# A gated MLP on one core: the fallback path rewritten as loops, another order for the last output tile, and fewer, wider warm-up matmuls

## The chip, the cores and the metric

The kernel runs on one NeuronCore of a Trainium2 chip. The metric is the device time of one execution in microseconds (us). The profile shows one execution, and its "span" runs from the first to the last recorded instruction of that execution. The time is some 1.5 to 1.9 us longer than the span, in four runs of one kernel (short, below) 2.1 to 2.7 us. The runs were made in several sessions, and the record names different chips for them; each ratio compares with runs of the kernel before of the same session. In the views, PE and PEld are TensorE's matmuls and weight loads, DVE is VectorE, ACT ScalarE, POOL GpSimd, and SPq the queue of SyncE, which issues most of the DMA transfers (80 of 86 in the kernel before). To evict a product is to copy it from the tile that TensorE wrote to the output tile `o`.

## The reference

```python
# x: 16 x 256 x 512, w1: 512 x 4096, w2: 2048 x 512, all float32, normal random numbers
h = x @ w1
gate, value = np.split(h, 2, axis=-1)
h = np.maximum(gate, 0) * value
return (h @ w2).astype(np.float32)
```

## The kernel before

The kernel has two ways through the work. The fast way computes everything in float16 with a seven-product scheme for 2 x 2 blocks (products P1 to P7), and at the same time sums squares of the inputs to decide whether float16 is fit for them. A branch at the end reads the verdict. With the inputs of this case it always jumps over the general way, which is therefore compiled but never executed.

```python
    with ExitStack() as fast:
        unfit = fast_way(fast, tc, x2, w1, w2, out2, flag)
    with tc.If(unfit > 0, label="general"):
        with ExitStack() as general:
            general_way(general, tc, x2, w1, w2, out2)
```

The general way is unrolled in Python: 8 chunks of 512 rows, each with 16 transposes, 128 first-layer matmuls and 64 second-layer matmuls.

```python
    for c in range(T // TH):                       # TH = 512
        xt = xp.tile([P, NK, TH], F32R, name="g_xt", tag="g_xt")
        for b in range(TH // P):
            t = xp.tile([P, D], F32, name="g_t", tag="g_t")
            nc.gpsimd.dma_start(out=t, in_=x2[c * TH + b * P:c * TH + (b + 1) * P, :])
            # ... 4 transposes and copies
        # ... for h in range(NH): 8 matmuls each;  for b in range(TH // P): 16 matmuls each, output by nc.gpsimd.dma_start
```

At its start, the fast way keeps TensorE busy on zeros while the first loads are under way. At its end, it computes the last of the four output tiles of the last 1,024 rows ("pair 3") in an order of its own. Each product that completes a quarter of an output is evicted by ScalarE or VectorE, and SyncE sends it.

```python
    for i in range(NWARM):                         # NWARM = 24
        nc.tensor.matmul(Y[:, :P], warm_b[:, :P], warm_b[:, :P], start=True, stop=True)
    nc.tensor.matmul(Y, warm_b[:, :P], warm_b, start=True, stop=True)
    # ...
    LAST_ORDER = ORDER.replace("P5 3, P2 3, P6 3, P3 3, P7 3", "P2 3, P6 3, P5 3, P7 3, P3 3")   # then P4 3
    # ...
            job(84, lambda: tc.mark_branch_hint_location("general", "LikelyTaken", [ENG.PE, ENG.DVE, ENG.SP]))
```

The last line asks for a hint that the branch around the general way will be taken. In the trace TensorE executes it once, at 0.82 us, some 300 us ahead of the branch.

## Time and profile before

| | |
|---|---|
| time, median of the first 3 runs | 308.26 us (307.19 to 308.72) |
| span of the profile | 307.2 us |
| last matmul ends | 303.03 us |
| tail: from there to the end of the span | 4.13 us |

The head and the chain of waits of the profile page of the kernel before:

```profile
span 307.2 us, 5283 instructions
...
PE 301.6 (98%) x1905; PEld 184.2 (60%) x1905; DVE 236.0 (77%) x388; ACT 176.3 (57%) x348; POOL 151.2 (49%) x189
...
PE 96%; DMA 2%; SPq 1%; issue 0%; ACT 0%
```

TensorE is the chain of waits, and nothing but the first microseconds and the last four can be moved by a change that leaves all products as they are.

The start of the timeline of the kernel before (start in us, length in us, engine, line, operation, tiles, and what the engine waited for):

```profile
0.24 0.10 POOL L774 MEMSET const-float32-0.0<- 128x1 f32 x1 [0.24 <-issue]
...
0.85 0.87 SPq L488 DMA_DIRECT2D x_A<-in_x_dram  x2
...
1.28 2.74 PE L148 MATMUL Y<-warm 128*128 128x128 f16 x24 [1.28 <-DVE warm L144]
```

The end of the timeline of the kernel before: the last eviction on ScalarE and the last three outputs issued by SyncE.

```profile
301.84 0.33 SPq L370 DMA_DIRECT2D out_dram<-o  x1
...
302.65 0.33 SPq L370 DMA_DIRECT2D out_dram<-o  x1
...
303.07 0.38 ACT L405 ACTIVATE o<-Y 128x256 f32<-128x256 f32 x1 [2.24 <-PE Y L362]
...
303.48 1.34 SPq L370 DMA_DIRECT2D out_dram<-o  x1
```

The last issue takes four times as long as the two before it. The DMA view of the kernel before, for 302 to 309 us (GB/s in 40 equal slices of 0.175 us; then queues with packets, MB and share; then issues with the time to landing):

```profile
GB/s 0 0 0 35 322 322 164 0 135 363 199 6 18 18 12 18 18 12 6 293 351 100 0 0 0 0 0 0 0 0 0 0 0 0 0 0 0 0 0 0
...
q8 instruction: 1, 0.02, 1.2%
q14 instruction: 1, 0.01, 0.4%
...
out_dram<-o SPq DMA_DIRECT2D x3, 128.0 KB, 2.7
```

Besides the outputs, there are instruction fetches, the packets of the queues that the view calls "instruction": one of 16 KB on queue 8 and one of 8 KB on queue 14. The trace's single packet records, below the views, place the 16 KB packet at 303.15 to 304.44 us. From 304 to 305.3 us the GB/s row shows 6 to 18 GB/s, where the outputs before and after it reach 351 to 363 in a slice. In the packet records, 14 of the 16 completion writes (packets of 4 bytes) of the output issued at 302.65 us come by 303.99 us, the last two at 304.73 and 305.14 us: as I read it, one or two late DMA engines are working off their packets alone. SyncE's closing wait for outputs, from the view of waits of SyncE's own queue in the same window (us in total, times, longest us):

```profile
SPq L785 <- DMA out_dram<-o: 0.4, 1, 0.4
```

### The profile page before, as it was taken

The page shows a single profiled execution, that of the slowest core. Times are in us where ns is not written, and L with a number is a line of the kernel's source. Part 1 is how long each engine was busy: PE and PEld are TensorE (multiplying, and loading weights), DVE is VectorE, ACT ScalarE, POOL GpSimd, SP SyncE. Part 2 cuts the span into 40 slices and gives each one's busy share as a digit, 9 for nine tenths or more (in the row PEclk, how much of TensorE's full clock was granted, in tenths as well). Part 3 has the DMA queues.
Part 4 walks back from the last instruction along what each step waited for, and adds up shares of the span by engine and source line. Part 5 has one row for each costly group of instructions (what it writes and reads, how often), then busy time and mean ns, then how long its engine had stood idle before and what let it go on. Part 6 is the DMA issues. An engine that isn't in the chain of part 4 may idle for free.

```text
span 307.2 us, 5283 instructions
## 1 busy us (share of the span) xinstructions
PE 301.6 (98%) x1905; PEld 184.2 (60%) x1905; DVE 236.0 (77%) x388; ACT 176.3 (57%) x348; POOL 151.2 (49%) x189
## 2 busy tenths in 40 slices
PE   8999999999999999999999999999999999999994
PEld 7744444588844444478864444458884444447883
DVE  2579888899778888887538888888536888888851
ACT  2488896455865555537855555546866555553231
POOL 2389999800068999300029889700007988700000
PEclk9999999999999999999999999999999999999999
DMA  6985779965775270001354910000325110001132
GB/s 204 358 259 179 239 171 176 229 123 80 260 209 88 69 137 3 0 0 55 136 182 108 207 34 2 0 2 9 130 101 174 35 34 0 3 1 34 54 106 87
DMA packets 35836, 32.87 MB, mean 107 GB/s; under 512 B 14432, under 2 KB 31328, under 8 KB 35680
## 3 DMA queue, kind: packets, MB, share of 16 engines
q1 hardware_dynamic: 33536, 26.22, 28.3%
q0 software_dynamic: 2272, 6.29, 11.4%
q8 instruction: 16, 0.26, 0.4%
q14 instruction: 12, 0.10, 0.1%
HBM read 27.26 MB, written 12.58 MB: 130 GB/s over the span
## 4 chain that ended last, share of the span: by engine, by line
PE 96%; DMA 2%; SPq 1%; issue 0%; ACT 0%
PE Y L250 26%; PE X L250 17%; PE W L250 17%; PE Y L362 14%; PE W L362 9%; PE X L362 9%; DMA x_A<-in_x_dram 2%; PE X L325 1%; PE W L325 1%; PE Y L325 1%; PE Y L498 0%; PE X L498 0%; SPq L217 0%; SPq L488 0%; ACT o L405 0%
## 5 line engine op out<-in xcount | busy, mean ns | idle before, releaser
L250 PEld LDWEIGHTS <-w_T 128*128 128x128 f16 x496 | 48.3, 98 | 57.3 <-POOL w_T L232 1.1
L179 POOL TENSOR_TENSOR fold<-xh 128x1024 f32<-128x1024 f16 x16 | 30.3, 1894 | 94.6 <-DMA xh<-x 93.7
L250 PE MATMUL X<-x_A,w_B 128*128 128x512 f16 x248 | 73.8, 379 | 0.0
L250 PE MATMUL Y<-x_S,w_T 128*128 128x512 f16 x220 | 65.5, 379 | 0.0
L250 PEld LDWEIGHTS <-w_B 128*128 128x128 f16 x372 | 36.3, 98 | 42.1
L277 DVE SCALAR_TENSOR_TENSOR cc<-W,pu 128x512 f32<-128x512 f32 x62 | 42.9, 691 | 21.1 <-ACT pu L271 21.1
L257 ACT COPY Y<-X 128x512 f32<-128x512 f32 x62 | 35.4, 571 | 38.2 <-PE X L250 37.9
L271 ACT ACTIVATE pu<-Y 128x512 f32<-128x512 f32 x62 | 37.1, 598 | 33.9 <-PE Y L250 33.0
L182 POOL TENSOR_TENSOR fold<-fold 128x512 f32<-128x512 f32 (+2 forms) x96 | 51.8, 539 | 7.5
L362 PEld LDWEIGHTS <-w_stage 128*128 128x128 f16 x512 | 50.0, 98 | 5.9
L287 DVE SCALAR_TENSOR_TENSOR cc<-Y,pu 128x512 f32<-128x512 f32 x62 | 42.9, 691 | 6.7
L282 DVE SCALAR_TENSOR_TENSOR g<-X,cc 128x512 f16<-128x512 f32 x62 | 42.8, 691 | 2.3
L299 DVE SCALAR_TENSOR_TENSOR g<-Y,cc 128x512 f16<-128x512 f32 x62 | 42.2, 681 | 1.8 <-PE Y L250 1.8
L362 PEld LDWEIGHTS <-g 128*128 128x128 f16 x384 | 37.5, 98 | 8.2
L264 ACT ACTIVATE pu<-W 128x512 f32<-128x512 f32 x62 | 37.2, 600 | 0.8 <-PE W L250 0.6
L250 PE MATMUL W<-x_S,w_B 128*128 128x512 f16 x124 | 36.9, 379 | 0.0
L250 PE MATMUL W<-x_S,w_T 128*128 128x512 f16 x124 | 36.9, 379 | 0.0
L250 PE MATMUL Y<-x_A,w_T 128*128 128x512 f16 x124 | 36.9, 379 | 0.0
L362 PE MATMUL X<-w,g 128*128 128x256 f16 x256 | 31.9, 273 | 0.0
L394 DVE SCALAR_TENSOR_TENSOR o<-W,pu 128x256 f32<-128x256 f32 x16 | 6.8, 423 | 19.4 <-PE W L362 19.4
L169 DVE TENSOR_TENSOR w_stage<-g 128x1024 f16<-128x1024 f16 x32 | 21.4, 684 | 0.2
L232 POOL TENSOR_TENSOR w_T<-w_stage 128x512 f16<-128x512 f32 (+1 forms) x16 | 18.7, 1173 | 2.5 <-DMA w_stage<-in_w_dram 2.5
(100 smaller groups left out, 307.5 us busy)
## 6 DMA issues: line engine op xcount, KB each, us to landing
w_stage<-in_w_dram SPq DMA_DIRECT2D x14, 512.0 KB, 6.0
out_dram<-o SPq DMA_DIRECT2D x26, 256.0 KB, 2.1
x<-in_x_dram POOLq DMA_DIRECT2D x4, 1024.0 KB, 9.1
xh<-x SPq DMA_DIRECT2D x16, 256.0 KB, 3.0
w<-in_w_dram POOLq DMA_DIRECT2D x2, 1024.0 KB, 10.2
out_dram<-o SPq DMA_DIRECT2D x12, 128.0 KB, 1.7
w_stage<-in_w_dram SPq DMA_DIRECT2D x4, 256.0 KB, 5.4
x_S<-in_x_dram SPq DMA_DIRECT2D x4, 256.0 KB, 6.5
```

The costliest lines, as they stand in the source:

```text
L169: eng.tensor_tensor(o[n], o[i0], o[i1], op=op)
L179: nc.gpsimd.tensor_tensor(fold, t, t, op=MULT)
L182: nc.gpsimd.tensor_tensor(fold[:, :, :m], fold[:, :, :m], fold[:, :, m:2 * m], op=ADD)
L250: nc.tensor.matmul(ps, wop[wn][:, b, self.jb * P:(self.jb + 1) * P], self.xo[xn][:, b, :], start=fresh and b == 0, stop=b == 1, skip_group ...
L257: nc.scalar.copy(out=self.Y, in_=self.X)
L264: nc.scalar.activation(self.p5, self.W, COPY, scale=GS)
L271: nc.scalar.activation(self.u2, self.Y, COPY, scale=GS)
L277: nc.vector.scalar_tensor_tensor(out=self.c12, in0=self.W, scalar=GS, in1=self.u2, op0=MULT, op1=ADD)
L282: nc.vector.scalar_tensor_tensor(out=self.g[:, self.jb, :TH], in0=self.X, scalar=0.0, in1=self.c12, op0=MAX, op1=MULT)
L287: nc.vector.scalar_tensor_tensor(out=self.c22, in0=self.Y, scalar=GS, in1=self.p5, op0=MULT, op1=ADD)
L299: nc.vector.scalar_tensor_tensor(out=self.g[:, self.jb, TH:], in0=self.Y, scalar=0.0, in1=self.c22, op0=MAX, op1=MULT)
L362: nc.tensor.matmul(ps, self.op[an][:, i], vop[wn][:, i], start=name in ("P1", "P5") and i == 0, stop=i == NJ // 2 - 1, skip_group_check=True)
```

## The change

Its intent was to make the code that is skipped small, to issue fewer TensorE instructions for the same warm-up time, and to send the last tile's outputs at better times. The diff, cut to its core:

```diff
-NWARM = 24
+NWARM = 4 * [TH] + 8 * [P]
 ... in general_way
-    for c in range(T // TH):
-        xt = xp.tile([P, NK, TH], F32R, name="g_xt", tag="g_xt")
+    xt = wp.tile([P, NK, TH], F32R, name="g_xt")
+    g = wp.tile([P, NH, TH], F32R, name="g_g")
+    with tc.For_i(0, T, TH) as row:
         for b in range(TH // P):
-            nc.gpsimd.dma_start(out=t, in_=x2[c * TH + b * P:c * TH + (b + 1) * P, :])
+            nc.gpsimd.dma_start(out=t, in_=x2[bass.ds(row + b * P, P), :])
 ...
-        for h in range(NH):
+        with tc.For_i(0, NH, 1) as h:
 ...
-            nc.gpsimd.dma_start(out=out2[c * TH + b * P:c * TH + (b + 1) * P, :], in_=o)
+            nc.gpsimd.dma_start(out=out2[bass.ds(row + b * P, P), :], in_=o)
 ... in fast_way
-    for i in range(NWARM):
-        nc.tensor.matmul(Y[:, :P], warm_b[:, :P], warm_b[:, :P], start=True, stop=True)
+    for n in NWARM:
+        nc.tensor.matmul(Y[:, :n], warm_b[:, :P], warm_b[:, :n], start=True, stop=True)
 ...
-    LAST_ORDER = ORDER.replace("P5 3, P2 3, P6 3, P3 3, P7 3", "P2 3, P6 3, P5 3, P7 3, P3 3")
+    LAST_ORDER = ORDER.replace("P5 3, P2 3, P6 3, P3 3, P7 3", "P6 3, P5 3, P7 3, P2 3, P3 3")
```

The output tile `o` is now allocated by whichever of P2 and P7 comes first.

## The prediction

> **What bounds it.** By the chain of waits TensorE is 96% of the span of 307.2 us, one DMA (x_A landing at 8.2 us) 2%. From 8.25 us to the last matmul's end at 303.03 us the timeline shows TensorE practically without gaps, so no product is saved. The change can only touch the head (8.2 us, bound by that load) and the tail: 4.1 us from the last matmul to the end of the span.

> **The tail, from the timeline and the raw instruction and packet records.** ScalarE's last eviction ends at 303.45; SyncE starts the last output's issue at 303.48, and that issue takes 1.34 us, where the two before it took 0.33 us. Its last packet is at 305.84 us, 2.36 us after the start of the issue; the two before needed 1.34 us. SyncE's closing waits and barriers add 1.3 us. What stands in the way: a 16 KB packet on the instruction queue, 303.15 to 304.44 us, right after TensorE's compare-and-branch (301.89 us) jumped over the unrolled general way. [...]packets of the output before are late as well (305.14 us). Likewise the issue at 299.11 took 1.04 us, fetch at 298.45.

> These fetches come about every 250 recorded TensorE instructions[...].

> **What the change does.**
> 1. Looped general way: never executed, but the code the branch skips shrinks on TensorE from some 3,300 instructions to about 200. I expect the target in the block already fetched, so the fetch at 303.15 us goes away. The last issue then takes 0.33 us instead of 1.34: about -1.0 us, all on the critical path.
> 2. Warm matmuls: 3,584 columns before and after (with the closing 512), so the same 2.9 us; 12 fewer pairs, 24 fewer TensorE instructions. The trace's full clock starts at 6.3 us, before the x_A load at 8.2. Direct gain 0. It shifts the block boundaries by 24 instructions: the last sequential fetch moves by 12 x 0.109 = 1.3 us, to about 299.8 us, and helps the branch and its target to share a block.
> 3. Last pair P6 P5 P7 P2 P3 P4: same products, same end of TensorE at 303.0. P6 follows the copy of X to Y with only P4 2 between; the copy ended at 297.37, P6 would start at 297.67, so no bubble. P2's output moves from 299.1 to about 301.7, P7's forward from 301.8 to about 300.97, away from the fetch; P3's and P4's stay. The last output decides, so 0 by itself.

> **Sum.** Span 307.2 to about 306.1 us if the late fetch goes (I give it two in three), unchanged if the branch still enters a new block. Predicted time 307.4 us, range 306.4 to 308.5 (the three runs of before spread over 1.5 us). Faster by over 2%: 0.02; within 2%: 0.965; slower by over 2%: 0.015.

> **Right or wrong in the profile.** Right: TensorE's last matmul again near 303.0; no 16 KB packet between 301 and 305 us; last output issue 0.33 us, landed 1.3 to 1.4 us after; 12 warm matmuls ending at the same time; no TensorE wait before P6. Wrong: last issue still over 1 us, or another engine's fetch in its place.

> **What would upset it.** Loops that add code for ScalarE or SyncE, whose branches then fetch late; more closing semaphore waits on SyncE; shifted block boundaries that put a fetch onto the first loads; a gap before P6.

Its sum: about -1.0 us for the late fetch, 0 for the warm matmuls and 0 for the order, so a span of about 306.1 us where it was 307.2. A "block" in it is what one 16 KB packet of instructions brings. Of its "two before" that needed 1.34 us, the records show that for the output issued at 301.84 us; the one issued at 302.65 us needed 2.50 us.

## The result, and the profile after

The kernel after took 308.90 us (median of 6 runs, 308.63 to 309.74), the kernel before 308.39 us (6 runs, 307.19 to 308.72). The ratio is 1.0025 with a 95% interval of 1.0004 to 1.0046: 0.25% slower. Ratios are the mean time of one kernel's runs over that of the other's of the same rounds, so not quite the ratio of the medians.

The same lines of the profile page of the kernel after:

```profile
span 308.2 us, 5263 instructions
...
PE 300.8 (98%) x1893; PEld 183.0 (59%) x1893; DVE 235.9 (77%) x388; ACT 176.4 (57%) x348; POOL 151.2 (49%) x189
...
PE 96%; DMA 2%; SPq 0%; POOL 0%; issue 0%; ACT 0%
```

Twelve matmuls fewer, as intended, and otherwise the same work. The start of the timeline of the kernel after:

```profile
0.47 0.10 POOL L782 MEMSET const-float32-0.0<- 128x1 f32 x1 [0.47 <-issue]
...
1.09 0.88 SPq L496 DMA_DIRECT2D x_A<-in_x_dram  x2
...
1.51 2.74 PE L151 MATMUL Y<-warm 128*128 128x512 f16 x12 [1.51 <-DVE warm L147]
```

The warm matmuls take the same 2.74 us. Everything starts 0.23 us later. The instruction records below the views show why: GpSimd now executes four register moves, 57 ns apart, from 0.19 to 0.40 us, ahead of its constants and of the start barrier, which SyncE passes at 0.89 us and TensorE at 0.90 us (0.66 and 0.67 before). They belong to the dynamic addresses of the loop's DMAs, which the kernel after has on GpSimd: in the kernel best, below, SyncE issues these DMAs, and four such moves stand at the start of SyncE's records instead.

The end of the timeline of the kernel after, the same four lines:

```profile
301.91 0.33 SPq L377 DMA_DIRECT2D out_dram<-o  x1
...
302.82 0.33 SPq L377 DMA_DIRECT2D out_dram<-o  x1
...
303.25 0.38 ACT L413 ACTIVATE o<-Y 128x256 f32<-128x256 f32 x1 [1.36 <-PE Y L365]
...
303.65 0.33 SPq L377 DMA_DIRECT2D out_dram<-o  x1
```

This is what the prediction hoped for: the last issue takes 0.33 us. (A second profile of the kernel before, below, shows 0.33 us too, so the 1.34 us was not there in every execution.) But the DMA view of 302 to 309 us of the kernel after shows where it was given back:

```profile
GB/s 310 328 76 0 222 345 182 0 0 164 328 211 29 6 222 439 147 0 0 47 0 12 6 12 12 23 23 6 0 0 0 0 0 0 0 0 0 0 0 0
...
q8 instruction: 1, 0.02, 0.8%
q14 instruction: 2, 0.02, 0.8%
...
out_dram<-o SPq DMA_DIRECT2D x3, 128.0 KB, 3.6
```

The time to landing grew from 2.7 to 3.6 us. The trickle of 6 to 23 GB/s, which stood between the last two outputs before, is now at the very end, from 305.7 to 306.7 us. And SyncE's closing wait for the outputs is five times as long:

```profile
SPq L793 <- DMA out_dram<-o: 2.0, 2, 1.7
```

The packet records of the end of the kernel after, from the raw trace (start in us, length in us, bytes):

```
304.796  0.928  16384   instruction queue
304.991  0.009      4   the 15th of the last output's 16 completion writes
305.710  0.124   1024   ┐
305.819  0.138   1024   │ sixteen output packets, one after another
 ...                    │
306.425  0.009      4   │ the output before is complete
 ...                    │
306.727  0.046   1024   ┘
306.770  0.009      4   the last output is complete
```

The records do not number the DMA engines, so the following is read from their order. Fifteen of the sixteen had finished at 304.99 us. The sixteenth carried a 16 KB instruction packet until 305.72 us and only then began on its share of both outputs, one packet at a time. The length of that packet is not all of its delay: the other fifteen had completed the output issued at 302.82 us by 304.55 us, before the 16 KB packet's record begins, and the sixteenth had moved nothing of it. What held it until 304.80 us no record shows. The tail is 4.98 us instead of 4.13.

By its size that packet is TensorE's: packets of 16,384 bytes come about every 250 recorded TensorE instructions (see the experiments). In the kernel before its compare-and-branch started at 301.89 us, took 0.50 us, and the 16 KB packet followed at 303.15. In the kernel after, the branch started at 301.19 us, took 1.96 us, and the packet followed at 304.80. The fetch that I expected to vanish had moved later, from ahead of the last output into the middle of it.

### The profile page after: what moved, and what is told of

It reads as the page before. It is cut to its first block, busy times and chain, and to the rows that moved or that the text cites. A ratio compares the mean times of both kernels' runs of the same rounds, so it can differ in the third digit from the quotient of the medians.

```text
span 308.2 us, 5263 instructions
## 1 busy us (share of the span) xinstructions
PE 300.8 (98%) x1893; PEld 183.0 (59%) x1893; DVE 235.9 (77%) x388; ACT 176.4 (57%) x348; POOL 151.2 (49%) x189
## 4 chain that ended last, share of the span: by engine, by line
PE 96%; DMA 2%; SPq 0%; POOL 0%; issue 0%; ACT 0%
PE Y L253 26%; PE X L253 17%; PE W L253 17%; PE Y L365 14%; PE X L365 9%; PE W L365 9%; DMA w_stage<-in_w_dram 2%; PE W L328 1%; PE X L328 1%; PE Y L328 1%; PE Y L506 0%; PE X L506 0%; SPq L496 0%; POOL w_T L474 0%; SPq L220 0%
## 5 line engine op out<-in xcount | busy, mean ns | idle before, releaser
(100 smaller groups left out, 305.3 us busy)
## 6 DMA issues: line engine op xcount, KB each, us to landing
w_stage<-in_w_dram SPq DMA_DIRECT2D x14, 512.0 KB, 6.2
```

## The experiments

Theory A: the time is lost at the end, where TensorE's instruction fetch after its branch (16 KB, 0.93 us long in the kernel after) occupies one DMA engine, and the three parts of the change matter only by where they put that fetch; in addition the register moves delay the head. Rival B: the new order of the last tile slows the tail. Rival C: the new warm matmuls delay the head.

### One part of the change alone: loops_only, order_only, warm_only

Edits: the kernel before with the new `general_way` alone, with the new `LAST_ORDER` (and the allocation of `o`) alone, and with the new `NWARM` alone.

```diff
 loops_only:  - for c in range(T // TH):   + with tc.For_i(0, T, TH) as row:     (the whole new general_way)
 order_only:  - "P2 3, P6 3, P5 3, P7 3, P3 3"   + "P6 3, P5 3, P7 3, P2 3, P3 3"
 warm_only:   - NWARM = 24   + NWARM = 4 * [TH] + 8 * [P]
```

> The kernel before with only the looped general way. Theory A (the head is late because GpSimd sets four registers, which its dynamic DMAs need, ahead of the start barrier; the tail is late because of where TensorE's instruction fetch after its branch falls): first warm matmul at 1.51 us instead of 1.28; the branch still at about 302 us, fetch of 16 KB at about 303.3, last output issue about 1.3 us long, tail from the last matmul to the end 4.1 us as before; in all +0.2 us. Rival B (the new order slows the tail) and rival C (the warm matmuls delay the head) expect no change from before at all: head 1.28 us, tail 4.1 us.

> The kernel before with only the last pair's new order. Theory A: head 1.28 us as before; P7's eviction ends early, so TensorE's sequencer reaches the branch at 301.0 instead of 301.9, the branch takes 1.5 to 2 us because its block came late (fetch near 300.2), and the fetch after it falls at 304 to 305 us, beside the last output: tail 4.6 to 5.0 us instead of 4.1, total +0.5 to +0.9 us. Rival B expects the same tail of 4.9 us but with no fetch needed for it: the last outputs late without a 16 KB packet beside them. Rival C: no change.

> The kernel before with only the new warm matmuls (24 TensorE instructions fewer ahead of the branch). Theory A: head 1.28 us as before; the block boundary is now crossed only after ScalarE has read P5's product (300.8 us), so the fetch of the branch's block comes at about 301.4 us, the branch at 301.9 waits until about 304, and the fetch after it comes at about 305.3 us, too late to hurt: last issue 0.33 us, last output landed at about 304.9, tail about 3.1 to 3.4 us, total -0.7 to -1.0 us. Rival C: head 0.2 us later, total +0.2. Rival B: no change.

Measured against the same 11 runs of the kernel before (median 308.48 us): loops_only 308.52 us, ratio 1.0003 (0.9989 to 1.0018). order_only 308.74 us, ratio 1.0019 (1.0002 to 1.0035). warm_only 309.54 us, ratio 1.0032 (1.0016 to 1.0047).

The warm matmuls, which add nothing to the head (first matmul at 1.28 us as before), are by the medians the dearest part (the intervals of warm_only and order_only overlap), and the loops, which do add 0.23 us to the head of the span, cost nothing measurable. The expectation for warm_only was wrong in sign: I had the fetches at 301.4 and 305.3 us, and they came at 300.98 and 304.07 us. At 305.3 the fetch would have missed the last output (an estimate: issued at 302.96 us, it would have landed near 304.4 us, at the 1.34 to 1.50 us that outputs without a later fetch needed); at 304.07 it met it, and the tail was 5.33 us, the longest of all. The mechanism of theory A fits, my forecast of its timing did not. Rivals B and C are both incomplete: the order costs something, and the warm matmuls cost without touching the head. Two more misses: order_only's tail was 4.06 us where 4.6 to 5.0 was expected, and loops_only's last issue took 1.04 us and its tail 3.81 us, where about 1.3 and 4.1 were.

### Take the fetch away: short

Edit: the kernel after, with the general way in turns of 128 rows instead of 512. It is never executed; in TensorE's stream the branch's target moves from instruction 4045 to 3922.

```diff
-    with tc.For_i(0, T, TH) as row:
-        for b in range(TH // P):
+    with tc.For_i(0, T, P) as row:
+        for b in range(P // P):
 ... and the tiles xt, g and v, gate and value are P wide
```

> The kernel after with a general way of 128 rows a turn instead of 512 (never executed): in the compiled TensorE stream the branch's target moves from instruction 4045 to 3922, which I place in the same 256-instruction block as the branch at 3803 (with an offset of about 64 read from the fetch times). Theory A: the branch takes under 0.1 us, no 16 KB packet after 301 us, last issue 0.33 us, last output landed about 305.0 us, tail 3.1 to 3.4 us; head still 1.51 us; total -0.7 to -1.0 us against before, 1.5 us under the kernel after. Rivals B and C: as the kernel after, tail 4.9 us.

Measured: the profile is as theory A says. TensorE's branch took 0.26 us (under 0.1 expected), no 16 KB packet lies between 287 us and the end of the span, the last output landed 1.36 us after its issue, and the tail is 3.16 us. Rivals B and C expected 4.9 us. The time gained less than expected: 308.16 us, ratio 0.9996 (0.9976 to 1.0016). Its mean span is 306.33 us against 306.68 us of the kernel before, and three of its six runs took 2.1 to 2.7 us more than their span, where the other three took 1.55 us.

### Is it the block boundary? pad_in and pad_out

Edit: the kernel short, with more matmuls in the skipped loop.

```diff
-            for h in range(NH):
+            for h in [*range(NH)] + 46 * [NH - 1]:     # pad_in;  58 in pad_out
```

Both kernels would compute nonsense in the general way; it is not executed, and their results are correct. The two differ in 24 TensorE instructions that never run.

> The kernel short with 46 more matmuls in the loop that is never executed: branch at instruction 3803, target at 4014 (short 3922, after 4045). With an offset of 64, read from the times of the fetches, the target stands at 4078, still ahead of the block boundary at 4096. Theory A (block boundary): as short, branch under 0.3 us, no 16 KB packet between 301 and 305 us, last output landed 1.3 to 1.4 us after its issue, tail 3.2 us. Rival (the length of the skipped code counts): halfway or nearer to after, tail about 4.5 us.

> As pad_in with 58 matmuls instead of 46, 24 TensorE instructions more, none of them executed: target at 4038, with the offset of 64 at 4102, just past the boundary at 4096. Theory A: as the kernel after: branch about 1.9 us, 16 KB packets near 300.4 and near 304 to 305 us, last landing 2 us or more after its issue, tail 4.2 to 5.0 us, some 1 us more than pad_in. Rival (length): the same as pad_in within 0.2 us.

Measured: pad_in 307.69 us (ratio 0.9983, 0.9964 to 1.0002), pad_out 308.25 us (ratio 1.0004, 0.9984 to 1.0023). By means of four runs each, 307.73 and 308.39 us: 0.66 us for 24 instructions that are not executed, and every run of pad_in (307.49 to 308.02) lies below every run of pad_out (308.19 to 308.86). The DMA view of 302 to 309 us of pad_in:

```profile
GB/s 88 339 299 24 0 29 339 304 88 12 94 345 287 47 47 0 0 0 0 0 0 0 0 0 0 0 0 0 0 0 0 0 0 0 0 0 0 0 0 0
...
q14 instruction: 2, 0.02, 0.8%
...
out_dram<-o SPq DMA_DIRECT2D x2, 128.0 KB, 2.2
```

Its closing wait, from the view of waits of SyncE's queue in the same window (us in total, times, longest us):

```profile
SPq L794 <- DMA out_dram<-o: 0.3, 1, 0.3
```

The DMA view of the same window of pad_out:

```profile
GB/s 328 334 47 0 0 351 357 88 18 47 310 299 59 82 12 12 23 23 6 0 0 0 0 0 0 0 0 0 0 0 0 0 0 0 0 0 0 0 0 0
...
q8 instruction: 1, 0.02, 1.1%
q14 instruction: 2, 0.02, 0.7%
...
out_dram<-o SPq DMA_DIRECT2D x2, 128.0 KB, 3.1
```

Its closing wait, from the view of waits of SyncE's queue in the same window (us in total, times, longest us):

```profile
SPq L794 <- DMA out_dram<-o: 1.2, 2, 1.0
```

The 16 KB packet on queue 8 is there in the one and not in the other, and with it come the trickle at the end and the longer wait. TensorE's branch took 0.26 us in pad_in and 1.80 us in pad_out. The rival, that the length of the skipped code counts, expected no difference. Theory A with an offset of about 64 is confirmed: the boundary lies between the two targets, so the offset is 58 to 81, and the target of the kernel after stands some 7 to 30 instructions beyond the boundary (13 by the estimate). The other way round, with VectorE's offset of 63 to 67 (itself reckoned with 128) the sixteenth block ends between 4078 and 4105, so a block has 254.9 to 256.6 instructions, which fits the estimate. But pad_out is not quite as the kernel after, as was expected: its later packet came at 302.93 us, not at 304 to 305, and its tail, 4.21 us, and its ratio are the smaller ones.

### The hint: short_unhinted and short_again

Edit of short_unhinted: the kernel short without TensorE's branch hint. short_again is the kernel short once more.

```diff
-            job(84, lambda: tc.mark_branch_hint_location("general", "LikelyTaken", [ENG.PE, ENG.DVE, ENG.SP]))
+            job(84, lambda: tc.mark_branch_hint_location("general", "LikelyTaken", [ENG.DVE, ENG.SP]))
```

> The kernel short without TensorE's branch hint (VectorE and SyncE keep theirs). In short the profile had no 16 KB packet from 287 us until 307.56 us, 1.7 us after the span had ended, and three of its six runs took 2.1 to 2.7 us more than their span where the others took 1.55. Theory A2 (the hint, pointing into the block that is already there, takes the place of the fetch of the next block, which the closing code after the span then misses): a 16 KB packet near 300.5 us again, none between 302 and 306 us, none near 307.6; tail 3.2 us; every run 1.5 to 1.6 us over its span; total 0.5 to 0.8 us under before. Rival: the excess of short is chance, and this kernel shows it too, with the 16 KB packet at 307.6 us.

> The same kernel as short, to see whether its excess over the span comes again. If TensorE's hint causes it: again some runs 2.1 us or more over their span. If it was chance (pad_in carries the same hint and had 1.52 to 1.59 in all four runs): all near 1.55 us, and the total 0.5 to 0.8 us under before.

Measured: short_unhinted 307.98 us, ratio 0.9982 (0.9966 to 0.9998), every run 1.52 to 1.69 us over its span, tail 3.11 us. The 16 KB packet near 300.5 us is back (300.53 to 301.47). So one part of A2 is shown: with the hint pointing into the block that TensorE is in (by the estimate), no 16 KB packet came from 287 us to the end of the span (short); without the hint one came at 300.53 us (short_unhinted). short_again took 308.07 us, ratio 0.9988 (0.9966 to 1.001), and one of its six runs was 2.35 us over its span. Four of twelve runs of the hinted kernel had an excess over 2.1 us, none of the six unhinted ones, but also none of the four of pad_in, which carries the hint. Whether the hint causes the excess stays open. The two profiles fit the other part of A2 without proving it: that of short is of a run 2.19 us over its span and shows a 16 KB packet at 307.56 us, after the span; that of short_again is of a run 1.55 us over, and shows none. No run takes the hint away where the target stands in another block.

### Take away the register moves as well: best

Edit: short, with SyncE issuing the two dynamic DMAs of the loop, and with no hints.

```diff
-            nc.gpsimd.dma_start(out=t, in_=x2[bass.ds(row + b * P, P), :])
+            nc.sync.dma_start(out=t, in_=x2[bass.ds(row + b * P, P), :])
-            nc.gpsimd.dma_start(out=out2[bass.ds(row + b * P, P), :], in_=o)
+            nc.sync.dma_start(out=out2[bass.ds(row + b * P, P), :], in_=o)
-            job(84, lambda: tc.mark_branch_hint_location(...))
```

> The kernel short, with the two DMAs of the skipped loop issued by SyncE instead of GpSimd (so the register moves that they need stand on SyncE, which waits 0.3 us at the start barrier anyhow), and with no branch hints. Theory A: start barrier released at 0.66 us as before, first output of SyncE at 0.75 to 0.80 us (0.85 before, 1.09 after) as its hint is gone too; first warm matmul at 1.28 us or a little less; tail 3.2 us with a 16 KB packet near 300 us and none from 302 us to the end; total 0.7 to 1.0 us under before (ratio 0.997). Rival (the register moves cost no measured time, because the time over the span shrank by 0.25 us in the looped kernels): total as short_unhinted.

Measured: 308.06 us, ratio 0.9991 (0.9974 to 1.0007). The head did move as expected: SyncE's first load is issued at 0.75 us (0.85 before, 1.09 after), the first warm matmul runs at 1.20 us. (Two things were changed at once, the moves and the hints.) The time did not follow. The mean span is 306.23 us, that of short_unhinted 306.20 us, and the time over the span is 1.83 us instead of 1.61. So the rival was right: the moves on GpSimd lengthen the head by 0.23 us, but I found no measured time that they cost. The kernels with them on GpSimd have a mean time over the span near 1.55 us (loops_only 1.54, kernel after 1.57, short_unhinted 1.61; short and short_again, with their excess, apart), all without near 1.8 us (order_only and warm_only 1.77, kernel before 1.80, best 1.83). What the time over the span consists of, no record shows.

### What the order and the warm matmuls are worth: short_alone and no_warm

Edits: short_alone is the kernel before with the general way of short and without TensorE's hint, so with the old order and the old warm matmuls. no_warm is the kernel after with `NWARM = 24 * [P]`.

> The kernel before with nothing changed but the skipped general way (128 rows a turn, looped) and TensorE's branch hint left out; the last pair's order and the warm matmuls are those of before. Branch at instruction 3826, target at 3945, with the offset of 64 at 4009, inside the block of the branch. Theory A: the new order and the new warm matmuls were worth nothing by themselves, so this is as fast as short_unhinted: no 16 KB packet between 301 us and the end, last issue 0.33 us, tail 3.1 to 3.5 us, total 0.5 to 0.8 us under before. P2's early output, issued at 298.9 us, may still meet the fetch at 298.5 and take 0.9 us to issue, which costs nothing. Rival (the order or the warm matmuls help once the fetch is gone): tail or total more than 0.3 us above short_unhinted's.

> The kernel after with the old 24 warm matmuls, so with the loops and the new order only. Theory A: the block of the target is fetched early again (near 299.9 us, as in order_only, because the boundary now falls ahead of P7's wait), the branch returns at about 302.8 us instead of 303.15, the fetch after it starts about 0.3 to 0.6 us after the last output's issue instead of 1.1 us, tail 4.0 to 4.4 us instead of 5.0; total 0.3 to 0.7 us under the kernel after, +0.1 to +0.5 against before. Rival (the new order is what costs, the warm matmuls nothing): as the kernel after, tail 4.9 us.

Measured: short_alone 308.37 us, ratio 0.9989 (0.9968 to 1.0009); no 16 KB packet after 299.9 us, last issue 0.33 us, landing after 1.45 us, tail 3.43 us. Its branch took 0.23 us. It is 0.32 us longer in the tail than short_unhinted, on the edge of what I had called a difference, and the intervals of the two ratios overlap, so these runs do not tell whether the order and the warm matmuls help a little once the fetch is gone.

no_warm: 308.85 us, ratio 1.001 (0.9993 to 1.0026). The block was fetched at 300.22 us, the branch returned at 302.66 us, the later fetch began at 303.42 us, 0.17 us after the last issue, and the tail is 4.20 us. That is below the 4.98 and 4.57 us (second profile, below) of the kernel after, as theory A expects, but it is one profile, and the intervals of the two times overlap: that the old warm matmuls are better with the new order is not shown.

### Does the shorter general way work? forced

Edit: short_alone with the bounds of the verdict exchanged (`HIGH, LOW = 32.0, 512.0`), so the general way always runs.

> short_alone with the two bounds of its verdict exchanged, so that the verdict always says unfit and the general way is executed after the fast one and writes every output again. Expected: a correct result (the general way of 128 rows works), and a far longer time, some hundreds of us more. It says nothing of the question of the tail.

Measured: the result is correct, in 3113.51 us, some 2,800 us more than without it, where I had expected some hundreds. The loops of 512 rows of the kernel after were never executed in any run.

### Second profiles: before_again, order_again, after_again

> The kernel before unchanged, for a second profile. If the tail of 4.13 us in the first profile is typical: 4.0 to 4.2 us. If it was a high one, as the spans of the timed runs suggest (mean 306.68 us against 307.16 in that profile): 3.6 to 3.9 us. In both cases the 16 KB packet starts 0.3 to 0.4 us ahead of the last output's issue and that issue takes about 1 us.

> order_only unchanged, for a second profile. It was 0.45 us slower than before in the timed runs but had no longer tail in its one profile (4.06 us). If the fetch is the cause: tail 4.0 us or more again, and above before_again's by 0.2 us or more; 16 KB packet 0.4 to 0.6 us after the start of the last output's issue.

> The kernel after unchanged, for a second profile; its first was that of its slowest run (span 308.2, the others 307.1 to 307.5). Branch about 1.9 us and a 16 KB packet after the start of the last output's issue in any case; tail between 4.2 and 5.0 us, above before_again's.

Measured: tails of 3.76, 4.39 and 4.57 us (times of 307.97, 308.56 and 308.86 us, one run each). So tails differ from run to run by some 0.4 us, but their order is the order of the times, and the 4.13 us of the first profile before was a high one. In before_again the issue took 0.33 us, not the 1 us that I expected, and its last output landed after 1.90 us: being ahead of the output by 0.24 us, the fetch held up the packets instead of the issue. In order_again the fetch came 0.07 us after the start of the issue, not 0.4 to 0.6.

### All runs side by side

All times in us. Times of instructions and packets are from the instruction and packet records of each run's one profile. "Block" is the last 16 KB packet that begins before TensorE's branch returns, "later" the one after that. "Landed" is counted from the start of the last output's issue.

| kernel | block | branch, start to return | later | last issue | landed | tail |
|---|---|---|---|---|---|---|
| before | 298.45 to 299.79 | 301.89 to 302.38 | 303.15 | 303.48 | +2.36 | 4.13 |
| before_again | 297.88 to 298.81 | 301.30 to 301.70 | 302.64 | 302.88 | +1.90 | 3.76 |
| loops_only | 298.48 to 299.43 | 301.66 to 302.16 | 302.90 | 303.25 | +2.05 | 3.81 |
| order_only | 299.82 to 301.24 | 300.59 to 302.69 | 303.58 | 303.05 | +2.17 | 4.06 |
| order_again | 299.44 to 300.77 | 300.38 to 302.20 | 302.92 | 302.84 | +2.53 | 4.39 |
| no_warm | 300.22 to 301.21 | 300.79 to 302.66 | 303.42 | 303.25 | +2.33 | 4.20 |
| pad_out | 299.83 to 300.78 | 300.41 to 302.22 | 302.93 | 302.88 | +2.35 | 4.21 |
| after_again | 299.92 to 300.94 | 300.64 to 302.37 | 303.83 | 303.10 | +2.70 | 4.57 |
| after | 300.53 to 301.71 | 301.19 to 303.15 | 304.80 | 303.65 | +3.12 | 4.98 |
| warm_only | 300.98 to 301.92 | 301.37 to 303.35 | 304.07 | 302.96 | +3.45 | 5.33 |
| pad_in | none | 300.56 to 300.83 | none | 303.03 | +1.42 | 3.37 |
| short | none | 300.72 to 300.98 | none | 303.19 | +1.36 | 3.16 |
| short_again | none | 300.60 to 300.86 | none | 303.07 | +1.42 | 3.24 |
| short_unhinted | 300.53 to 301.47 | 301.20 to 301.44 | none | 303.67 | +1.34 | 3.11 |
| best | 300.20 to 301.08 | 300.78 to 301.01 | none | 303.24 | +1.50 | 3.47 |
| short_alone | 298.56 to 299.88 | 301.85 to 302.08 | none | 303.44 | +1.45 | 3.43 |

Two regularities can be read from it. First, without a later fetch the last output lands after 1.34 to 1.50 us, with one after 1.90 to 3.45 us, and the later the fetch starts relative to the issue (0.35 us ahead of it up to 1.14 us behind it), the worse it is on the whole. Second, where the branch had to wait for its block, it took 1.73 to 2.10 us, against 0.40 to 0.50 us where that packet had landed before the branch started (before, before_again, loops_only) and 0.23 to 0.27 us with the target in the branch's own block (the last six lines), and it returned 1.43 to 1.45 us after the end of that block's packet (order_only, order_again, no_warm, pad_out, after_again, after, warm_only). So in these seven profiles the later the block, the later the branch's return, and the next fetch comes behind that. In all ten profiles with a later packet it begins only after the branch has returned, and TensorE executes instructions behind the target before it lands (in the kernel after its DRAIN of L793 at 303.40 us, the packet from 304.80 us), so it does not bring the target; what it holds, no record tells. This is how parts that leave the products alone moved the tail:

- The order brings P7 forward. The records show the branch 0.07 us after the end of P7's eviction on VectorE, at 301.19 instead of 301.89 us, so it starts before its block has arrived (301.71 us) instead of after.
- The block is fetched later. Counted back from the end of the last matmul, its packet starts 4.6 us ahead in both profiles of the kernel before, 1.5 us ahead with the 24 warm instructions fewer alone (warm_only), and 2.8 and 3.0 us ahead with the new order alone (order_only, order_again). Once the order is new, the 24 instructions make no clear difference: 2.7 us in both profiles of the kernel after, 2.6 us in no_warm.
- The loops bring the target from far away to some 13 instructions past the boundary by the estimate, which is still a new block, and the fetch stays (302.90 us in loops_only, 303.15 and 302.64 us before).

One link stays open. From the branch's return to the later packet pass 0.72 to 0.94 us in eight profiles, but 1.65 and 1.46 us in the two of the kernel after. pad_out has the same order, the same warm matmuls and a target just past the boundary too, and shows 0.72 us. So part of the delay of the fetch in the kernel after, some 0.8 us, has no cause that these runs show.

## Why the prediction was right or wrong

It was wrong: 307.4 us predicted (306.4 to 308.5), 308.9 us measured, and the sign of the difference was missed.

What held: TensorE is the chain of waits, the change touches only head and tail, all products keep their times, the warm matmuls take the same time, the new order causes no gap ahead of P6, and the last issue takes 0.33 us. The last sequential fetch came near the time that was said (299.8 us predicted, 300.53 us measured, in a profile whose last matmul is 0.18 us later), but by luck: the prediction put the shift down to the 24 warm instructions, and the new order alone brings that fetch to 299.82 us (order_only). The class, within 2%, was right.

The step that failed is step 1: "I expect the target in the block already fetched, so the fetch at 303.15 us goes away." The target is some 13 instructions beyond the end of the branch's block, by the estimate that pad_in and pad_out bear out. A block fetched ahead was not enough: a 16 KB packet started at 300.53 us, before the branch at 301.19, and the later fetch came all the same. The prediction had also taken the later fetch for that of the branch's target, but in the kernel before the branch had returned at 302.38 us, and TensorE executed a closing instruction behind the target (DRAIN of L785) at 303.22 us, while the packet landed only at 304.44. The fetch did not go away; it started at 304.80 us (303.83 in the second profile) and now the last output's packets came late instead of its issue. In place of the 1.0 us gained (a size read from one profile, whose 1.34 us issue did not come again in the second), the tail grew by 0.8 us (mean of two profiles: 4.77 us after, 3.94 us before). pad_in and pad_out show that such a step can hang on 24 instructions, and short shows what it would have been worth in the tail had it held: about 0.8 us (3.16 against 3.94 us).

Steps 2 and 3 were each booked with 0. Alone they cost 0.32% (warm_only) and 0.19% (order_only). The prediction saw that the boundary shifts by 24 instructions and that the outputs move, but not that an earlier branch (301.19 instead of 301.89 us) and a later block (landed at 301.71 instead of 299.79 us) make the branch wait (1.96 instead of 0.50 us), and that the wait carries the following fetch towards the last output (in the kernel after further than these runs explain).

A term was missing as well: the 0.23 us of register moves at the head of the span. It is shown by the records, but the time over the span shrank by the same amount, so it explains none of the measured loss. Adding up: tail +0.83 us, head +0.23 us, time over the span -0.23 us, together +0.83 us, against +0.77 us from the ratio (0.0025 x 308.4).

The timed gain of the kernels without the late fetch is smaller than the tail promises. The fastest, short_unhinted and pad_in, are 0.17 to 0.18% under the kernel before, some 0.55 us; only short_unhinted's interval excludes 1, just, and it is one of eleven such intervals. By its mean it beats both kernels, narrowly.

## What to carry to other kernels

Code that is skipped still had its place in the instruction stream: 24 instructions that never run made 0.66 us (pad_in against pad_out). In ten of the sixteen profiles an instruction packet of 16 KB began behind the branch over that code, 0.35 us ahead to 1.14 us behind the last output's issue, and the output landed 1.90 to 3.45 us after its issue instead of 1.34 to 1.50. When the tail matters, look at the packet records behind the last output for 16 KB packets on an instruction queue and for packets that come one after another long after the others (305.71 to 306.77 us in the kernel after, the rest done by 305.00), and try to put the branch and its target into one block, or the fetch clear of the last output. Count instructions before trusting a change that only "shortens" code: here, shorter brought nothing until the target was on the near side of the boundary (loops_only 1.0003; pad_in 0.9983 against pad_out 1.0004), and changes elsewhere that add or drop a few instructions moved the fetch too (24 fewer at the start of the kernel: from 4.6 us to 1.5 us ahead of the last matmul's end in warm_only).
